# Attention in head pairs with the forget gate added by VectorE, in a two-layer hybrid trunk

## Chip, cores, metric

The kernel runs on one NeuronCore of a Trainium2 chip. The metric is the device time of one execution in microseconds; a kernel is described by the median of its runs.

## What is computed

x is 256 x 1024, in fp32. Layer 0 is an FFN, a gated linear recurrence (RG-LRU) and an FFN; from its result K, V and a forget gate are projected once; layer 1 is an FFN, attention on that K and V, and an FFN. Every block has a norm before and behind it. The change touches the shared K and gate and the attention:

```python
def shared_kv(h, g, w_kv, w_f, b_f):
    hn = rms_norm(h, g)
    kv = (hn @ w_kv).reshape(Bn, S, 2, N_HEADS, HEAD_DIM)          # 16 heads of 64
    ...
    log_f = jax.nn.log_sigmoid((hn @ w_f + b_f).astype(jnp.float32))
    c = jnp.cumsum(log_f, axis=1).transpose(0, 2, 1)
    return k, v, c

def forgetting_attention(xq, w_q, w_o, k, v, c):
    q = (xq @ w_q).reshape(...).transpose(0, 2, 1, 3) * (HEAD_DIM ** -0.5)
    for blk in range(S // Q_BLOCK):                                # two halves of 128 tokens
        ...
        logits = logits + c[:, :, q0:end, None] - c[:, :, None, :end]
        logits = jnp.where(kpos[None, :] <= qpos[:, None], logits, -jnp.inf)
        p = jax.nn.softmax(logits, axis=-1).astype(v.dtype)
        outs.append(jnp.einsum('bhqk,bhkd->bhqd', p, v[:, :, :end]))
    return o @ w_o
```

## The kernel before

**Split products.** Each fp32 weight block of 128 x 1024 is loaded (`load_raw`, five raw buffers, issued by SyncE) and split into an upper part (whi, ScalarE, L199) and a rest (wlo, VectorE, L200), nine such units deep. A product is three matmuls: upper by upper, upper by rest, rest by upper. `mm3` (L207 to L209) does it with the activations still and 512 weight columns moving, once for each half of 128 tokens. `mmj` (L222, L223) does it with 128 x 128 of the weights still and the activations of both token halves moving: 512 columns (upper and rest side by side), then 256. `still` and `tile_items` run `mmj` over four PSUM banks at a time, lent from the pool; `total` then adds the two halves of the banks (a ScalarE copy and a VectorE add).

**Order.** TensorE's order is written out by hand; the order on the other engines is that of a scheduler. A slot is the work of one unit for one token half (six matmuls of 512 columns in the projections). Each slot counts down a list of deferred calls (`defer(n, fn)`), and each prepares the next units.

**PSUM.** `pall` is 8 banks of 128 x 512: 0 to 3 for products, 4 and 5 for logits and small things (`gtbank`), 6 and 7 for transposes (`trbank`). `sparebank` takes what is not lent.

**K and V.** V comes first, in three column blocks, with the 16 gate columns (`v_items`); `running` makes the cumulative gate c (`cq`, and `nck` = -c) out of it. Then K, in two column halves by `proj_items` with L207 to L209 (96 matmuls). `heads_T` (L1015 to L1027) scales a 128 x 512 block into `htok`, puts two more columns beside the 64 of a head (a one, and -c), and transposes four heads at a time into kT, 66 rows high. Q goes the same way, with c and a one, so that the 66-row product of the logits adds the gate by itself.

**Attention.** `attention(t)` is written for a token half t. Half 0 has 4 groups of 4 heads (128 keys), half 1 has 8 groups of 2 heads (256 keys). Step i issues `logits(i)` (L1128, then VectorE's mask L1129 and max L1131, then ScalarE's exps L1136 with their sums), `values(i - 3)` (L1155), `turn(i - 2)` (transposes of the weights pe, L1144, copied to pT by ScalarE, L1146) and, behind every eight heads, `output` (transposes of the normalised result `ot`, L1160 and L1168, split into oh and ol, L1171 and L1172). Successive groups of logits use banks 4 and 5 in turn. The steps are woven into the slots of Q and of the output projection w_o by `ATT_ORDER`: "0" and "1" are slots of a token half, "a0" and "a1" steps of the attention:

```python
    ATT_ORDER = ("0 0 0 0 0 0 0 0 a0 1 a0 1 1 1 a0 1 a0 1 a0 1 a0 a1 1 a0 "
                 "0 a1 a0 a1 0 a1 0 a1 0 a1 0 a1 0 a1 0 a1 0 a1 1 a1 1 a1 1 1 1 1 1 1")
```

The last FFN, ffn_d, follows. L699 is a transpose of the recurrence's parameters, a call deferred by 40 slots in the first FFN.

## Time and profile before

| | us |
|---|---|
| median of 3 runs | 1008.35 (1008.03 to 1010.38) |
| the profiled execution | 1007.29 |
| its span, first to last instruction | 1005.6 |
| TensorE busy | 991.0 |
| VectorE busy | 665.3 |
| ScalarE busy | 566.1 |

TensorE works for nearly the whole span at the full granted clock (mean 0.999). A matmul's record is longer than its distance to the next, since matmuls overlap: costs on TensorE are read from start to start. In the trace a 4-byte matmul of the logits and values counts as two instructions (x8 for four heads).

### The profile page before, as it was taken

To read this page: it belongs to the slowest core of one execution; us is meant where nothing else is said; L and a number is where in the kernel's file an instruction comes from. 1 tells how busy PE (TensorE), PEld (TensorE's weight loads), DVE (VectorE), ACT (ScalarE), POOL (GpSimd) and SP (SyncE) were. 2 spreads that over 40 slices of the span, in tenths; PEclk is the share of its full clock that TensorE was granted. 3 is DMA by queue.
4 is the path that set the end of the run, shared out by engine and by line. 5 is a ranking of instruction groups with operands and counts; after the bars stand their busy time and mean duration, and the time that the engine had idled before them with its cause. 6 is when DMAs were issued, how large, how long until landed. Compare 5 with 4: busy or idle time off the path is not lost.

```text
span 1005.6 us, 13910 instructions
## 1 busy us (share of the span) xinstructions
PE 991.0 (99%) x5302; PEld 847.3 (84%) x5302; DVE 665.3 (66%) x768; ACT 566.1 (56%) x742; POOL 51.5 (5%) x113
## 2 busy tenths in 40 slices
PE   8999999999999999999999999999999999999997
PEld 5887888889988888888898888888888888888885
DVE  5877664568998676664695577674477477666642
ACT  5656543559987555543565555553468566555431
POOL 1500000000003000000000000000020020000000
PEclk9999999999999999999999999999999999999999
DMA  6877656565427666545476766655555057665431
GB/s 230 280 263 204 190 161 197 154 181 151 141 78 250 212 188 187 188 158 185 114 227 218 209 191 184 192 189 168 168 168 168 2 188 237 184 199 195 155 121 42
DMA packets 91864, 178.90 MB, mean 178 GB/s; under 512 B 11790, under 2 KB 31318, under 8 KB 91798
## 3 DMA queue, kind: packets, MB, share of 16 engines
q1 hardware_dynamic: 90550, 176.89, 56.8%
q10 hardware_dynamic: 608, 1.06, 0.3%
q8 instruction: 41, 0.67, 0.3%
q0 software_dynamic: 640, 0.07, 0.1%
q14 instruction: 25, 0.20, 0.1%
HBM read 176.95 MB, written 1.05 MB: 177 GB/s over the span
## 4 chain that ended last, share of the span: by engine, by line
PE 70%; issue 21%; ACT 4%; DVE 4%; POOL 1%; DMA 0%; DVEq 0%; POOLq 0%; ACTq 0%
PE pall L222 21%; PE pall L223 11%; PE pall L209 10%; PE pall L208 10%; PE pall L207 10%; PE pall L845 1%; DVE wlo L200 1%; PE pall L214 1%; PE pall L215 1%; PE pall L216 1%; PE pall L1128 1%; ACT junk L236 1%; PE pall L1155 1%; ACT whi L199 1%; PE pall L1026 1%
## 5 line engine op out<-in xcount | busy, mean ns | idle before, releaser
L200 DVE TENSOR_TENSOR wlo<-raw,whi 128x1024 fp32r<-128x1024 f32 (+4 forms) x329 | 394.6, 1206 | 242.3 <-ACT whi L199 241.8
L199 ACT ACTIVATE whi<-raw 128x1024 fp32r<-128x1024 f32 (+4 forms) x329 | 342.1, 1044 | 290.3 <-PE pall L209 125.6
L222 PE MATMUL pall<-xall,whi 128*128 128x512 f32 x1216 | 424.7, 395 | 0.0
L223 PE MATMUL pall<-xall,wlo 128*128 128x256 f32 x1216 | 338.4, 278 | 0.0
L222 PEld LDWEIGHTS pall<-xall,whi 128*128 128x128 f32 x1216 | 228.1, 188 | 53.3
L223 PEld LDWEIGHTS pall<-xall,wlo 128*128 128x128 f32 x1216 | 228.8, 188 | 0.2
L207 PE MATMUL pall<-whi,hhi 128*128 128x512 f32 (+2 forms) x432 | 166.0, 384 | 0.0
L209 PE MATMUL pall<-whi,hlo 128*128 128x512 f32 (+2 forms) x432 | 165.0, 382 | 0.0
L208 PE MATMUL pall<-wlo,hhi 128*128 128x512 f32 (+2 forms) x432 | 164.8, 382 | 0.0
L209 PEld LDWEIGHTS pall<-whi,hlo 128*128 128x128 f32 x432 | 81.1, 188 | 15.1
L208 PEld LDWEIGHTS pall<-wlo,hhi 128*128 128x128 f32 x432 | 81.2, 188 | 14.7
L207 PEld LDWEIGHTS pall<-whi,hhi 128*128 128x128 f32 x432 | 81.2, 188 | 14.6
L207 PE MATMUL pall<-whi,xall 128*128 128x512 f32 (+2 forms) x168 | 67.1, 400 | 0.1
L208 PE MATMUL pall<-wlo,xall 128*128 128x512 f32 (+2 forms) x168 | 64.9, 386 | 0.4 <-DVE wlo L1226 0.2
L209 PE MATMUL pall<-whi,xall 128*128 128x512 f32 (+2 forms) x168 | 64.9, 386 | 0.1
L229 POOL TENSOR_SCALAR nv<-ss 128x1 f32<-128x1 f32 x24 | 10.9, 453 | 749.8 <-ACT junk L236 749.6
L208 PEld LDWEIGHTS pall<-wlo,xall 128*128 128x128 f32 x168 | 31.7, 189 | 7.5 <-DVE wlo L200 1.2
L209 PEld LDWEIGHTS pall<-whi,xall 128*128 128x128 f32 x168 | 31.5, 188 | 7.1 <-DVE xall L259 1.1
L207 PEld LDWEIGHTS pall<-whi,xall 128*128 128x128 f32 x168 | 31.6, 188 | 5.7 <-ACT xall L254 0.5
L567 ACT ACTIVATE hhi<-prod 128x1024 fp32r<-128x1024 f32 (+1 forms) x21 | 20.6, 980 | 25.2 <-DVE prod L563 25.2
L300 DVE SCALAR_TENSOR_TENSOR t<-pall,rstd,gb 128x512 f32<-128x512 f32 x16 | 11.9, 748 | 26.7 <-ACT junk L236 26.7
L557 ACT ACTIVATE sil<-sil 128x1024 f32<-128x1024 f32 (+1 forms) x21 | 20.6, 982 | 15.1 <-DVE sil L556 15.0
(190 smaller groups left out, 974.2 us busy)
## 6 DMA issues: line engine op xcount, KB each, us to landing
raw<-in_ffn_w_down_dram SPq DMA_DIRECT2D x88, 512.0 KB
raw<-in_ffn_w_up_dram SPq DMA_DIRECT2D x80, 512.0 KB
raw<-in_ffn_w_gate_dram SPq DMA_DIRECT2D x79, 512.0 KB
raw<-in_rg_w_in_dram SPq DMA_DIRECT2D x20, 504.0 KB
raw<-in_rg_w_out_dram SPq DMA_DIRECT2D x10, 504.0 KB
raw<-in_ffn_w_gate_dram SPq DMA_DIRECT2D x18, 256.0 KB
raw<-in_ffn_w_up_dram SPq DMA_DIRECT2D x16, 256.0 KB
raw<-in_w_kv_dram SPq DMA_DIRECT2D x8, 512.0 KB
```

What stands on the lines that cost most here:

```text
L199: nc.scalar.activation(hi[:parts, c:c + m], rawv[:, c:c + m], AF.Copy)
L200: nc.vector.tensor_tensor(lo[:parts, c:c + m], rawv[:, c:c + m], hi[:parts, c:c + m].bitcast(F32), ALU.subtract)
L207: nc.tensor.matmul(ps, xh, wh, start=first, stop=False)
L208: nc.tensor.matmul(ps, xh, wl, start=False, stop=False)
L209: nc.tensor.matmul(ps, xl, wh, start=False, stop=last)
L214: nc.tensor.matmul(ps, wh, xh, start=first, stop=False)
L222: nc.tensor.matmul(pall[:, b, :], wh, xall[:, k, :, :].rearrange("p a b -> p (a b)"), start=k == 0, stop=False)
L223: nc.tensor.matmul(pall[:, b, :S], wl, xhi[:, k, :], start=False, stop=k == 7)
L229: nc.gpsimd.tensor_scalar(v, ss[:, 0:1], ss[:, 1:2] if n == 2 else 0.0, D * EPS * f * f, ALU.add, ALU.add)
L300: nc.vector.scalar_tensor_tensor(t1[n], pf[n], r_in, gb[:, n * 512:(n + 1) * 512], ALU.mult, ALU.mult)
L557: nc.scalar.activation(s, s, AF.Silu)
L567: nc.scalar.activation(hv, pv, AF.Copy)
```

## The change

K is projected by `tile_items`: weights still, the activations z of both halves moving (for that the hidden tile of ffn_b becomes one tile, `hid["all"]`), first into banks 4 to 7 and then into 0 to 3; `total` and a VectorE multiply by the row of norms write kT, now 128 rows (two heads one above the other) by 8 pairs. K is not transposed. Q is transposed in blocks of 128 columns, two heads at a time. The gate no longer rides in the product: `rows(t)` transposes -c, SyncE writes it to a scratch in DRAM and reads it back spread over 128 partitions into `nb` (two DMAs of 128 x 16 x 128, one for each half of the keys; GpSimd then masks the upper half), and VectorE adds c and nb to each head's logits in one operation (L1167). Logits are 64-row matmuls, the two heads of a pair in the two row halves of the array, the one into bank 4 and the other into bank 5, columns 0 to 255 or 256 to 511 in turn. The softmax weights are divided by their sums on VectorE (L1181) before they are turned; in `values` v stands still in column halves and pT moves, so the result comes out transposed and is split into oh and ol (L1207, L1208) at once: `output` and its step go. The recurrence's parameters wait four slots longer.

```diff
--- before
+++ after
     def mmj(b, wh, wl, k, moving):
...
+        both, upper = moving(k)
...
+        nc.tensor.matmul(o, wh, both, start=k == 0, stop=False)
+        nc.tensor.matmul(oh, wl, upper, start=False, stop=k == 7)
...
+    def total(v, b, m):
+        nc.scalar.activation(v, pall[:, b:b + m, S:], AF.Copy)
+        nc.vector.tensor_tensor(v, pall[:, b:b + m, :S], v, ALU.add)
...
-    def heads_T(pool, ps, t, n, scale, cols, dst):
-        if n + t == 0:
-            toks["h"] = pool.tile([P, 16 * HA], F32, tag="prod", name=nm("htok"), bufs=1).rearrange("p (t a b) -> p t a b", t=2, a=8)
-        tok = toks["h"][:, t, :, :]
-        nc.vector.tensor_scalar(tok[:, :, :HD], ps.rearrange("p (a b) -> p a b", a=8), rs[t][:, 0:1], scale,
-                                ALU.mult, ALU.mult)
-        for c, col in enumerate(cols):
-            if col is None:
-                nc.gpsimd.memset(tok[:, :, HD + c:HD + c + 1], 1.0)
-            else:
-                nc.gpsimd.tensor_copy(tok[:, :, HD + c:HD + c + 1], col[:, 8 * n:8 * n + 8].unsqueeze(2))
-        def turn(b):
-            tp = sparebank()
+    def heads_T(pool, ps, t, n, scale, dst):
+        tok = pool.tile([P, 512], F32, tag="htok", name=nm("htok"), bufs=2)
+        nc.vector.tensor_scalar(tok, ps, rs[t][:, 0:1], scale, ALU.mult, ALU.mult)
+        def turn():
+            tp = trbank()
             for j in range(4):
-                nc.tensor.transpose(tp[:HA, j * P:(j + 1) * P], tok[:, 4 * b + j, :], ident)
-            nc.scalar.activation(dst[:, 8 * n + 4 * b:8 * n + 4 * b + 4, :],
-                                 tp[:HA, :].rearrange("p (a b) -> p a b", a=4), AF.Copy)
-        defer(2, lambda: turn(0))
-        defer(3, lambda: turn(1))
+                nc.tensor.transpose(tp[:, j * P:(j + 1) * P], tok[:, j * P:(j + 1) * P], ident)
+            nc.scalar.activation(dst[:, 4 * n:4 * n + 4, :].rearrange("p a b -> p (a b)"), tp, AF.Copy)
+        defer(2, turn)
     def post_k(n):
-        return lambda t, ps: heads_T(pools["f"], ps, t, n, 1.0, (None, kv["nck"][t]), kv["kT"][:, :, t * P:(t + 1) * P])
+        def f(b, m):
+            kk = pools["f"].tile([P, 16 * HA], F32, tag="prod", name=nm("kk"), bufs=1)[:, :1024]
+            v = kk.rearrange("p (a b) -> p a b", a=4)
+            total(v, b, m)
+            nc.vector.tensor_tensor(kv["kT"][:, 4 * n:4 * n + 4, :], v, rcp["v"].unsqueeze(1).to_broadcast([P, 4, S]), ALU.mult)
+        return f
+    def z_moving(k):
+        return kv["z"][:, :, :, k, :], kv["z"][:, 0, :, k, :]
...
     def running(t):
-        pc = gtbank()
+        pc = sparebank()
         if t == 1:
             nc.tensor.matmul(pc[:, :NH], kv["ones"], kv["lf"][0], start=True, stop=False)
         nc.tensor.matmul(pc[:, :NH], kv["triu"], kv["lf"][t], start=t == 0, stop=True)
         nc.vector.tensor_copy(kv["cq"][t], pc[:, :NH])
         nc.vector.tensor_scalar(kv["nck"][t], pc[:, :NH], -1.0, None, ALU.mult)
+        defer(3, lambda: rows(t))
+    def rows(t):
+        pc = sparebank()
+        nc.tensor.transpose(pc[:NH, :P], kv["nck"][t], ident)
+        nc.vector.tensor_copy(kv["ckT"][:, t * P:(t + 1) * P], pc[:NH, :P])
+        if t == 1:
+            nc.sync.dma_start(kv["dram"], kv["ckT"])
...
-        proj_items(A["w_kv"], n * 512, 512, z_x, post_k(n))
+        tile_items(A["w_kv"], n * 512, 4 - 4 * n, post_k(n), z_moving)
...
+        nb = att["nb"] = ap.tile([P, NH, S], F32, name="nb")
+        src = kv["dram"].rearrange("h k -> (h k)").partition_broadcast(P).rearrange("p (h k) -> p h k", h=NH)
+        for k in range(2):
+            nc.sync.dma_start(nb[:, :, k * P:(k + 1) * P], src[:, :, k * P:(k + 1) * P])
+        nc.gpsimd.affine_select(out=nb[:, :, P:], in_=nb[:, :, P:], compare_op=ALU.is_ge, fill=NEG, base=0,
+                                pattern=[[0, NH], [-1, P]], channel_multiplier=1)
+        att["q"] = [ap.tile([P, 8, P], F32, name=f"qT{t}") for t in range(2)]
         ap.tile([P, 32], F32, name="pad")
...
         per = 4 // nk
-        mask = kv["cmask"].unsqueeze(1).to_broadcast([P, per, P])
+        np_ = per // 2
+        w = nk * P
         box = {}
         G = NH // per
+        def head(hg, b, j):
+            return 2 * (hg * np_ + j) + b
         def logits(hg):
-            hds = range(hg * per, (hg + 1) * per)
-            ps = gtbank().rearrange("p (a b) -> p a b", a=per)
-            for j, hd in enumerate(hds):
-                nc.tensor.matmul(ps[:, j, :], att["q"][t][:, hd, :], kv["kT"][:, hd, :nk * P], start=True, stop=True)
-            nc.vector.tensor_tensor(ps[:, :, t * P:], ps[:, :, t * P:], mask, ALU.add)
-            mx = spool.tile([P, 4], F32, tag="mx", name=nm("mx"))
-            nc.vector.tensor_reduce(mx[:, :per], ps, AX.X, ALU.max, negate=True)
-            if hds[0] % 8 == 0:
-                box["sm"] = spool.tile([P, 8], F32, tag="sm", name=nm("sm"))
-            pe = ap.tile([P, per, nk * P], F32, tag="pe", name=nm("pe"), bufs=3)
-            for j, hd in enumerate(hds):
-                nc.scalar.activation(pe[:, j, :], ps[:, j, :], AF.Exp, bias=mx[:, j:j + 1],
-                                     accum_out=box["sm"][:, hd % 8:hd % 8 + 1])
-            box["pe", hg], box["s", hg] = pe, box["sm"]
+            c = (hg % 2) * S
+            lg = pall[:, 4:6, c:c + S]
+            for j in range(np_):
+                for b in range(2):
+                    p = hg * np_ + j
+                    nc.tensor.matmul(lg[:, b, j * w:(j + 1) * w], att["q"][t][b * HD:(b + 1) * HD, p, :],
+                                     kv["kT"][b * HD:(b + 1) * HD, p, :w], start=True, stop=True)
+            for b in range(2):
+                for j in range(np_):
+                    hd = head(hg, b, j)
+                    v = lg[:, b, j * w:(j + 1) * w]
+                    nc.vector.scalar_tensor_tensor(v, v, kv["cq"][t][:, hd:hd + 1], att["nb"][:, hd, :w], ALU.add, ALU.add)
+            if t == 0:
+                v = lg.rearrange("p b (j k) -> p b j k", j=2)
+                nc.vector.tensor_tensor(v, v, kv["cmask"].unsqueeze(1).unsqueeze(1).to_broadcast([P, 2, 2, P]), ALU.add)
+            mx = spool.tile([P, 4], F32, tag="mx", name=nm("mx"))[:, :per]
+            nc.vector.tensor_reduce(mx, lg.rearrange("p b (j k) -> p b j k", j=np_), AX.X, ALU.max, negate=True)
+            sm = spool.tile([P, 4], F32, tag="sm", name=nm("sm"))[:, :per]
+            pe = box["pe", hg] = ap.tile([P, per, w], F32, tag="pe", name=nm("pe"), bufs=3)
+            for b in range(2):
+                for j in range(np_):
+                    i = b * np_ + j
+                    nc.scalar.activation(pe[:, i, :], lg[:, b, j * w:(j + 1) * w], AF.Exp, bias=mx[:, i:i + 1],
+                                         accum_out=sm[:, i:i + 1])
+            nc.vector.reciprocal(sm, sm)
+            nc.vector.tensor_tensor(pe, pe, sm.unsqueeze(2).to_broadcast([P, per, w]), ALU.mult)
         def turn(hg):
             tp = trbank()
             nc.scalar.activation(pT.rearrange("p a b -> p (a b)"), tp, AF.Copy)
         def values(hg):
-            hds = range(hg * per, (hg + 1) * per)
-            if hds[0] % 8 == 0:
+            p0 = hg * np_
+            if p0 % 4 == 0:
                 box["po"] = mmbank()
-            po, pT, sm = box["po"], box["pT", hg], box["s", hg]
-            for j, hd in enumerate(hds):
+            po, pT = box["po"], box["pT", hg]
+            for j in range(np_):
+                o = (p0 + j) % 4 * P
                 for k in range(nk):
-                    nc.tensor.matmul(po[:, (hd % 8) * HD:(hd % 8 + 1) * HD], pT[:, j * nk + k, :],
-                                     kv["v"][k][:, hd * HD:(hd + 1) * HD], start=k == 0, stop=k == nk - 1)
-            if hds[-1] % 8 == 7:
-                nc.vector.reciprocal(sm, sm)
-                ot = box["ot", hds[-1] // 8] = ap.tile([P, 8, HD], F32, tag="ot", name=nm("ot"), bufs=2)
-                nc.vector.tensor_tensor(ot, po.rearrange("p (a b) -> p a b", a=8),
-                                        sm.unsqueeze(2).to_broadcast([P, 8, HD]), ALU.mult)
+                    for b in range(2):
+                        hd = head(hg, b, j)
+                        nc.tensor.matmul(po[b * HD:(b + 1) * HD, o:o + P], kv["v"][k][:, hd * HD:(hd + 1) * HD],
+                                         pT[:, (b * np_ + j) * nk + k, :], start=k == 0, stop=k == nk - 1)
+            if (p0 + np_) % 4 == 0:
+                b = (p0 + np_) // 4 - 1
+                oh_v = att["oh"][t][:, 4 * b:4 * b + 4, :].rearrange("p a b -> p (a b)")
+                ol_v = att["ol"][t][:, 4 * b:4 * b + 4, :].rearrange("p a b -> p (a b)")
+                nc.scalar.activation(oh_v, po, AF.Copy)
+                nc.vector.tensor_tensor(ol_v, po, oh_v.bitcast(F32), ALU.subtract)
                 release(po)
-        def output(b):
-            otv = box["ot", b].rearrange("p a b -> p (a b)")
-            tp = trbank()
-            for j in range(4):
-                nc.tensor.transpose(tp[:, j * P:(j + 1) * P], otv[:, j * P:(j + 1) * P], ident)
-            oh_v = att["oh"][t][:, 4 * b:4 * b + 4, :].rearrange("p a b -> p (a b)")
-            ol_v = att["ol"][t][:, 4 * b:4 * b + 4, :].rearrange("p a b -> p (a b)")
-            nc.scalar.activation(oh_v, tp, AF.Copy)
-            nc.vector.tensor_tensor(ol_v, tp, oh_v.bitcast(F32), ALU.subtract)
         steps = []
-        for i in range(G + 4):
+        for i in range(G + 3):
             s = []
             if i < G:
                 s.append(lambda i=i: logits(i))
                 s.append(lambda i=i: values(i - 3))
             if 0 <= i - 2 < G:
                 s.append(lambda i=i: turn(i - 2))
-            j = i - 4
-            if j >= 0 and (j + 1) * per % 8 == 0:
-                s.append(lambda j=j: output((j + 1) * per // 8 - 1))
             steps.append(s)
         return steps
...
-                 "0 a1 a0 a1 0 a1 0 a1 0 a1 0 a1 0 a1 0 a1 0 a1 1 a1 1 a1 1 1 1 1 1 1")
+                 "0 a1 0 a1 0 a1 0 a1 0 a1 0 a1 0 a1 0 a1 1 a1 1 a1 1 1 1 1 1 1")
...
-    defer(40, rg_params)
+    defer(44, rg_params)
...
-    run(n_kv)
+    run_ffn((n_v, n_kv, n_kv))
```

### Where it moves instructions

First place: TensorE in the first token half. Before, from the first logits (L1128) to the second; kT and qT are K and Q transposed, whi, wlo and xall the operands of a slot.

```order
L1128 MATMUL pall<-kT,qT_6471 128x128 x4
L207 MATMUL pall<-whi_6282,xall 128x512
L208 MATMUL pall<-wlo_6283,xall 128x512
L209 MATMUL pall<-whi_6282,xall 128x512 [waits DVE_49]
...
L1128 MATMUL pall<-kT,qT_6471 128x128 [waits Activation_49]
L1128 MATMUL pall<-kT,qT_6471 128x128 x3
```

The wait of the second logits here is for the copy into qT. After, the same stretch:

```order
L1161 MATMUL pall<-kT,qT_6470 128x128 [waits Activation_49]
L1161 MATMUL pall<-kT,qT_6470 128x128 x3
L207 MATMUL pall<-whi_6275,xall 128x512
L208 MATMUL pall<-wlo_6276,xall 128x512
L209 MATMUL pall<-whi_6275,xall 128x512 [waits DVE_49]
...
L1161 MATMUL pall<-kT,qT_6470 128x128 [waits DVE_49,Activation_49]
L1161 MATMUL pall<-kT,qT_6470 128x128 [waits Activation_49]
L1161 MATMUL pall<-kT,qT_6470 128x128 x2
```

The qT of both is written ahead of the first logits now; the waits of the second on ScalarE are for the second and the fourth exp of the first group, which read the banks that these matmuls write.

Second place: VectorE between the max of the second group (mx) and that of the third. Before:

```order
L1131 TENSOR_REDUCE mx_6602<-pall 128x4 [waits DVE_49]
L1158 RECIPROCAL sm_6579<-sm_6579 128x8 [waits Activation_49]
L1015 TENSOR_SCALAR htok_6527<-pall,rstd_6517 128x8x64 [waits PE_49,Pool_49]
L200 TENSOR_TENSOR wlo_6625<-raw_6622,whi_6624 128x1024 [waits DMAHW1_49,Activation_49]
L1129 TENSOR_TENSOR pall<-pall,cmask 128x512 [waits PE_49]
L200 TENSOR_TENSOR wlo_6642<-raw_6639,whi_6641 128x1024 [waits DMAHW2_49,Activation_49]
L200 TENSOR_TENSOR wlo_6657<-raw_6654,whi_6656 128x1024 [waits DMAHW4_49,Activation_49]
L1131 TENSOR_REDUCE mx_6665<-pall 128x4 [waits DVE_49]
```

After:

```order
L1172 TENSOR_REDUCE mx_6603<-pall 128x4 [waits DVE_49]
L200 TENSOR_TENSOR wlo_6629<-raw_6626,whi_6628 128x1024 [waits DMAHW2_49,Activation_49]
L1180 RECIPROCAL sm_6605<-sm_6605 128x4 [waits Activation_49]
L1181 TENSOR_TENSOR pe_6606<-pe_6606,sm_6605 128x512 [waits DVE_49]
L1027 TENSOR_SCALAR htok_6650<-pall,rstd_6516 128x512 [waits PE_49,Pool_49]
L200 TENSOR_TENSOR wlo_6641<-raw_6638,whi_6640 128x1024 [waits DMAHW6_49,Activation_49]
L200 TENSOR_TENSOR wlo_6655<-raw_6652,whi_6654 128x1024 [waits DMAHW7_49,Activation_49]
L1167 SCALAR_TENSOR_TENSOR pall<-pall,cq_2932,nb 128x128 [waits PE_49] x2
L1167 SCALAR_TENSOR_TENSOR pall<-pall,cq_2932,nb 128x128 [waits DVE_49] x2
L200 TENSOR_TENSOR wlo_6692<-raw_6689,whi_6691 128x1024 [waits DMAHW0_49,Activation_49]
L1170 TENSOR_TENSOR pall<-pall,cmask 128x2x256 [waits DVE_49]
L1172 TENSOR_REDUCE mx_6667<-pall 128x4 [waits DVE_49]
```

Between the two maxima stand now a multiply, four gate adds and one split more.

Third place: TensorE at the start of the second half of K, after the change (whi and wlo are units of K, hid holds z; before, slots of L207 to L209 with blocks of L1026 stood here).

```order
L233 MATMUL pall<-hid_3062,wlo_4710 128x256
L232 MATMUL pall<-hid_3062,whi_4722 128x512 [waits Activation_49]
L233 MATMUL pall<-hid_3062,wlo_4723 128x256
L232 MATMUL pall<-hid_3062,whi_4722 128x512
...
L232 MATMUL pall<-hid_3062,whi_4722 128x512 [waits DVE_49]
...
L1076 MATMUL pall<-ident,nck_2931 16x128 [waits DVE_49]
L232 MATMUL pall<-hid_3062,whi_4722 128x512
```

The transpose of the second `rows` stands behind eight matmuls of the second half, in a bank out of which `total` still adds the first half (its wait on VectorE).

More of the change, by code (lines that the diff above doesn't have):

```diff
@@ L545, in post_up @@
             return f
-        def total(v, b, m):
-            nc.scalar.activation(v, pall[:, b:b + m, S:], AF.Copy)
-            nc.vector.tensor_tensor(v, pall[:, b:b + m, :S], v, ALU.add)
         def gate_rows(b, m):
@@ L604, in work @@
                 def work(t, u, k0=k0):
[L605 removed]
+                    still(u, k0, 4)
                     if k0 == 6:
```

71 lines of the change are left out of this document (40 added, 31 removed).

## The prediction

> **What bounds the kernel now.** I read the busy lines first, then TensorE's waits, then the stretches of the attention, then single rows.
>
> ```profile
> PE 991.0 (99%) x5302; PEld 847.3 (84%) x5302; DVE 665.3 (66%) x768; ACT 566.1 (56%) x742; POOL 51.5 (5%) x113
> PE pall L699 <- issue: 2.1, 1, 2.1
> ...
> PE pall L1155 <- ACT pT L1146: 0.3, 1, 0.3
> ```
>
> TensorE is busy for 99% of a span of 1005.6 us. In the second view (us in total, times, longest us) the attention owns one wait of 0.3 us: it costs only what TensorE executes. So the change can gain by removing matmuls and by the 2.1 us at L699, and it loses whatever it makes TensorE wait for. The next table (stretch, length, busy us of PE, PEld, DVE, ACT, POOL, granted clock, DMA share, GB/s) covers the attention:
>
> ```profile
> 745.00:765.00 20.00, 20.00 (x127) 17.31 (x126) 12.04 (x16) 14.24 (x38) 0.24 (x2) 1.00 0.33 99
> 765.00:785.00 20.00, 19.93 (x128) 17.30 (x128) 13.06 (x21) 13.33 (x38) 0.24 (x2) 1.00 0.43 133
> 785.00:805.00 20.00, 19.69 (x125) 17.42 (x124) 8.51 (x15) 10.83 (x29) 0.87 (x2) 1.00 0.00 1
> ```
>
> VectorE and ScalarE work 43 to 71% of the time there, unnoticed, because each softmax has some microseconds of matmuls to hide behind. The sum below is made against this execution's 1007.29 us; the median of the runs, 1008.35, is 1.1 us above it, and I add the sum to the median.
>
> **The change, part by part.**
>
> A. The gate's parameter transpose (L699) stands 33 matmuls later.
>
> ```profile
> 82.01 0.39 PE L222 MATMUL pall<-xall,whi 128*128 128x512 f32 x1
> ...
> 82.36 0.39 PE L222 MATMUL pall<-xall,whi 128*128 128x512 f32 x1
> ...
> 85.00 0.27 PE L699 MATMUL pall<-ident,prow 88*126 88x88 f32 x1 [2.13 <-issue]
> ```
>
> A pair L222 + L223 takes 0.35 us (82.01 to 82.36), so 33 matmuls are 5.8 us, more than the wait: **-2.1**. If the wait only moved, 0.
>
> B. K with still weights. 96 matmuls of 0.23 us (start to start, as from 748.91 to 749.14 under D) become 64 pairs of 0.35 us: 22.1 against 22.4, +0.3. Eight blocks of four transposes go:
>
> ```profile
> 755.53 0.60 PE L1026 MATMUL pall<-ident,htok 128*66 128x128 f32 x4
> 755.88 0.47 PE L207 MATMUL pall<-whi,xall 128*128 128x512 f32 x1
> ```
>
> 0.35 us to the next start, and that matmul is 0.09 us longer than usual: 8 x 0.44 = -3.5. Two small transposes (rows(t)) cost some 0.3. But the second stands behind only eight matmuls (1.4 us) of the second half of K, and it writes into a bank that the first half of K still holds. It waits for VectorE's add, and the order shows what lies ahead of that: on ScalarE a split that starts only when the last-but-one matmul of the first half is done, then the copy; on VectorE the split of the same unit, then the add.
>
> ```profile
> L199 ACT ACTIVATE whi<-raw 128x1024 fp32r<-128x1024 f32 x284 | 299.4, 1058 | 272.7 <-PE pall L209 115.6 <-PE pall L222 96.7 <-issue 46.6
> L549 ACT ACTIVATE prod<-pall 128x1024 f32<-128x1024 f32 x17 | 17.2, 1009 | 1.8 <-PE pall L223 1.8
> L200 DVE TENSOR_TENSOR wlo<-raw,whi 128x1024 fp32r<-128x1024 f32 x284 | 345.5, 1222 | 229.5 <-ACT whi L199 229.0
> L550 DVE TENSOR_TENSOR prod<-pall,prod 128x1024 f32<-128x1024 f32 x17 | 20.7, 1217 | 1.6 <-ACT prod L549 1.6
> ```
>
> 1.06 + 1.22 + 1.22 = 3.5, minus 1.4: a new stall of 2.1 (0.8 if the split is early: 1.01 + 1.22 - 1.4). B together: **-0.8** (-2.1 to -0.6).
>
> C. Q's transposes: two blocks per 512 columns become one. One such block less stands ahead of the first logits: **-0.4**. The other savings of this kind lie inside D, where a wait decides.
>
> D. First token half. Up to now logits of successive groups went to alternate banks. Now each group writes both banks 4 and 5, and the order shows logits(i+1) waiting for the exps of group i; six matmuls stand between. That takes away the cover on which the 99% rest. Rows of before, TensorE and ScalarE:
>
> ```profile
> 748.91 0.39 PE L209 MATMUL pall<-whi,xall 128*128 128x512 f32 x1
> 749.14 1.05 PE L1128 MATMUL pall<-kT,qT 66*128 66x128 f32 x8
> 749.95 0.48 PE L207 MATMUL pall<-whi,xall 128*128 128x512 f32 x1
> ...
> 751.42 1.06 PE L1128 MATMUL pall<-kT,qT 66*128 66x128 f32 x8
> ...
> 757.40 1.16 PE L1128 MATMUL pall<-kT,qT 66*128 66x128 f32 x8
> ...
> 760.22 1.05 PE L1128 MATMUL pall<-kT,qT 66*128 66x128 f32 x8
> ...
> 769.36 1.03 PE L1128 MATMUL pall<-kT,qT 66*128 66x256 f32 x4
> ...
> 793.24 1.03 PE L1128 MATMUL pall<-kT,qT 66*128 66x256 f32 x4
> ```
>
> ```profile
> 751.62 1.06 ACT L199 ACTIVATE whi<-raw 128x1024 fp32r<-128x1024 f32 x1 [3.07 <-PE pall L209]
> 752.69 1.28 ACT L1136 ACT_TABLE_LOAD   x1
> 753.99 0.37 ACT L1136 ACTIVATE pe<-pall,mx 128x128 f32<-128x128 f32 x1
> ...
> 755.28 0.21 ACT L1136 ACTIVATION_READ_ACCUMULATOR pe<-pall,mx 128x1 f32 x1
> ```
>
> Before, the exps of group 0 ran from 4.85 to 6.35 us after logits(0) began (T = 749.14), and logits(1) started at +2.28, four microseconds before they were done. The same split and table load stand before them in the changed order, so logits(1) cannot end before +6.8 (before +3.1). VectorE's part fits in that time; its prices:
>
> ```profile
> L803 DVE SCALAR_TENSOR_TENSOR xc<-pall,par,xc 126x255 f32<-126x255 f32 x10 | 4.7, 472 | 0.0
> L300 DVE SCALAR_TENSOR_TENSOR t<-pall,rstd,gb 128x512 f32<-128x512 f32 x16 | 11.9, 748 | 26.7 <-ACT junk L236 26.7
> L1129 DVE TENSOR_TENSOR pall<-pall,cmask 128x512 f32<-128x512 f32 x4 | 2.8, 695 | 1.0 <-PE pall L1128 0.9
> L1131 DVE TENSOR_REDUCE mx<-pall 128x2 f32<-128x512 f32 x8 | 5.5, 688 | 0.2
> L1160 DVE TENSOR_TENSOR ot<-pall,sm 128x512 f32<-128x512 f32 x4 | 2.8, 689 | 1.4 <-PE pall L1155 1.4
> L1136 ACT ACTIVATE pe<-pall,mx 128x256 f32<-128x256 f32 x16 | 7.4, 471 | 1.1 <-DVE mx L1131 1.1
> ```
>
> ```profile
> 756.92 0.20 DVE L1158 RECIPROCAL sm<-sm 128x8 f32<-128x8 f32 x1 [1.98 <-ACT pe L1136]
> ```
>
> No row has the new gate add. Between 255 columns (0.47) and 512 (0.75) lies a slope that gives 0.34 for 128 columns and 0.47 for 256; I bound it by 0.30 (the same line through the mask) and 0.47. Group 1: multiply of group 0 until +7.25, four adds 1.36, mask 0.70, reduce 0.69 until +10.0, four exps until +11.6; then the next qT copy (0.6), for which logits(2) wait: **+12.2** against +8.26 before. Logits(3) wait for the exps of group 2, and VectorE has ahead of those: split 1.22, reciprocal and multiply until +12.5, htok 0.75, two splits 2.44, four adds 1.36, another split 1.22, mask and reduce 1.38: +19.6; the first two exps end at +20.5, the others at +21.2. TensorE has been out of work since +14.8. Logits(3) are at **+20.5** against +11.08. To the first logits of the other token half there remain 7.6 us of matmuls and about 1 us of waiting for pT and the multiply: **+29.5** against +20.22 before. D: **+9.2** (+6 to +11; the low end if the three splits find their way around the chain, as the order denies).
>
> E. Second half, eight groups. VectorE's order per group is reciprocal, add, multiply, add, reduce: 0.20 + 0.47 + 0.69 + 0.47 + 0.69 = 2.5; with the exps ahead (0.47 + 0.47 + 0.21) the ring closes after 3.65, plus 0.69 where an ol split stands in it. Before, the seven distances add up to 23.88 (769.36 to 793.24), two of them short since nothing chained them. Now 4.6 for the first (12 matmuls stand there as before), 3.9, and five of 3.65 + 0.69: 27.5. E: **+3.6** (0 to +5; at 0 the adds run below the rows).
>
> F. Behind the last logits two blocks of output transposes go (-0.9, by the 0.44 of B), and values in column halves may run side by side:
>
> ```profile
> 764.42 1.00 PE L1155 MATMUL pall<-v,pT 128*128 128x64 f32 x8
> 765.26 0.61 PE L1144 MATMUL pall<-ident,pe 128*128 128x128 f32 x4
> ```
>
> Eight such passes take 0.84 us to the next start, so halves side by side save 0.42 per block, four blocks 1.6; I take half of it and 0.5 us for a wait on the direct oh and ol: **-1.2** (+0.5 to -2.5).
>
> Whether halves run side by side no row shows: a pass of 64 columns (105 ns) is no shorter than one of 128 (101 ns, 749.14 to 749.95 for eight), so serial halves cost what full passes did. The Trainium skill, "TensorEngine Tiling (Array Packing)", Key Properties, says that tiles run in parallel, but also that changing the tiling mode drains the TensorE; no run here shows that. By the first half the sum would be 2 to 3 us lower, by the second higher, as rival 4 works out.
>
> Sum: -2.1 - 0.8 - 0.4 + 9.2 + 3.6 - 1.2 = **+8.3** on 1007.29 (1015.6), on the median 1008.35: **1016.6**, rounded to 1016.5.
>
> **Rivals.**
>
> 1. *The waits are covered and the matmuls decide.* L699 -2.1; B without its stall -2.9; eight Q blocks become four, -1.8; four blocks of output transposes, -1.8; halves of the logits up to -5 and of the values -5: about -19, **989**. For it: TensorE is at 99%, so every matmul counts. Against it: the exps of group 0 end at +6.35 in a row of before, and the order makes logits(1) wait for them. Chance 0.05. With half the waiting of D and E, -6.4: -6 less some halves, about **1001 to 1006**, 0.15.
>
> 2. *The spread tile is late* (the slower end). SP issues it behind ffn_c's last matmul, some 13.6 us ahead of the first add (735.75 to 749.99, less C and some), and the w_o weights and the gain queue behind it.
>
> ```profile
> 735.75 0.39 PE L209 MATMUL pall<-whi,hlo 128*128 128x512 f32 x1
> ```
>
> ```profile
> q1 hardware_dynamic: 90550, 176.89, 56.8%
> ```
>
> 90550 packets hold 16 engines for 571 us each, so 0.10 us for a packet of 1950 bytes. The tile is 4096 rows of 512 bytes: by packets 26 us, by bytes 6.7. At the first price the w_o weights land some 5 us after ScalarE needs them, and their splits stand ahead of pT and the exps in its order: **1021**. It decides from about 0.06 us per packet. Chance 0.15.
>
> 3. *The clock drops in the pauses.* In the pause of 2.13 us at L699 the granted clock stays 1.00; D has one of 3.3 us (+2.3 to +5.6, where two exps are done) and one of 5.7, longer than any here. Half a clock for as long as the pause lasted would cost 1.5 to 3 us: **1019**. The Trainium skill, "TensorE: Matmul & The Clock Gate", What's actually happening, has the clock halve after an idle window of about 3.4 us; L699 agrees as far as it goes. Chance 0.1.
>
> 4. *Each change between full and half tiles empties TensorE.* Twelve logits and twelve values blocks change it and change it back, 48 changes; by what a matmul outlasts its pitch (0.39 - 0.23 = 0.16) 7.7 us, of which the waits of D and E hide the half that belongs to the logits: +3.8, **1020**. No row speaks for or against it. Chance 0.05.
>
> **How the numbers follow.** Forecast 0.5 (1011 to 1020, at 1016.5); rival 2 0.15; rival 3 0.1; rival 4 0.05; rival 1 0.05 and its milder form 0.15. The range, 1004 to 1023, leaves out rival 1's full form, the lower half of the milder one, and a sum of several of 2 to 4. A measurement of this kernel tells about 0.3% (3 us) from no change: faster than 1005.3, 0.05 and 0.08 of the milder form; from there to 1011.4 the rest of it and 0.06 of the forecast, 0.13; slower, 0.74.
>
> **What would show it.** A: no wait at L699. B: a wait of about 2 us at L1076 on VectorE's add. D: waits at L1161 on ScalarE's pe, together 8 to 10 us, the longest, 5 to 6 us, before logits(3). E: logits of the second half 3.6 to 4.4 us apart. If TensorE's waits at L1161 add up to less than 3 us I am wrong about the banks; if ScalarE's L199 waits for DMAs around the first logits, rival 2; if the clock column falls below 1.00 there, rival 3. It would be wrong altogether if the waits are there and the end still comes earlier: then halves side by side saved more than I gave them.

## The result, and the profile after

The changed kernel takes 1024.33 us (median of three runs, 1021.49 to 1026.52) against 1009.36 us before: ratio 1.0147, 95% interval 1.0110 to 1.0183. It is slower by about 15 us, where 8 were forecast and the range ended at 1023. A fourth run, the one that was profiled, had 0.84 of the clock from end to end (1103.77 us) and is left out, so the lines below come from a second profile of the same kernel (run `again`: 1022.86 us, span 1021.1).

Its busy line and TensorE's waits (us in total, times, longest):

```profile
PE 993.4 (97%) x5272; PEld 839.6 (82%) x5272; DVE 682.6 (67%) x810; ACT 563.0 (55%) x732; POOL 49.1 (5%) x98
PE pall L1161 <- ACT pe L1178: 12.0, 5, 4.9
PE pall L1076 <- DVE kk L517: 2.0, 1, 2.0
PE pall L151 <- DVE idle L137: 1.5, 1, 1.5
PE pall L232 <- DVE ckT L1077: 1.2, 1, 1.2
```

The wait at the parameter transpose is gone from the list. In its place stand 12.0 us ahead of logits, on ScalarE's exps, and two waits in K, of which one was forecast (L1076, 2.0 against 2.1) and one was not (L232).

The logits of the changed kernel (start, duration, the idle time ahead and what ended it), first half and the first and last of the second:

```profile
747.94 0.72 PE L1161 MATMUL pall<-kT,qT 64*128 64x128 f32 x8
...
753.51 1.92 PE L1161 MATMUL pall<-kT,qT 64*128 64x128 f32 x8 [3.27 <-ACT pe L1178]
...
762.07 0.72 PE L1161 MATMUL pall<-kT,qT 64*128 64x128 f32 x8
...
769.66 1.91 PE L1161 MATMUL pall<-kT,qT 64*128 64x128 f32 x8 [4.90 <-ACT pe L1178]
...
780.68 0.70 PE L1161 MATMUL pall<-kT,qT 64*128 64x256 f32 x4
...
808.06 1.67 PE L1161 MATMUL pall<-kT,qT 64*128 64x256 f32 x4 [2.09 <-ACT pe L1178]
```

Counted from the first logits they stand at +5.6, +14.1, +21.7 and +32.7 (before +2.3, +8.3, +11.1, +20.2). Look at the durations too: eight passes take 0.72 us in two of the rows and 1.9 in the other two, the ones behind a pause. The table of stretches says why (the third column from the right is the granted clock):

```profile
745.00:765.00 20.00, 16.50 (x78) 12.32 (x76) 12.81 (x22) 10.37 (x26) 2.02 (x1) 0.83 0.48 161
765.00:785.00 20.00, 15.29 (x84) 11.02 (x84) 14.27 (x26) 10.52 (x30) 0.00 (x0) 0.83 0.43 131
785.00:805.00 20.00, 18.27 (x104) 12.08 (x105) 13.32 (x30) 8.50 (x26) 0.00 (x0) 1.00 0.10 28
805.00:825.00 20.00, 17.80 (x103) 13.16 (x100) 12.22 (x21) 11.45 (x24) 1.89 (x5) 0.83 0.12 30
```

Three of the four have lost 17% of their clock. In stretches of one microsecond, around the first pause:

```profile
752.00:753.00 1.00, 0.00 (x0) 0.00 (x0) 0.59 (x1) 0.99 (x3) 0.00 (x0) 0.84 0.00 0
753.00:754.00 1.00, 0.49 (x2) 0.49 (x2) 0.00 (x0) 1.00 (x8) 0.00 (x0) 0.50 0.63 74
...
758.00:759.00 1.00, 1.00 (x6) 0.92 (x5) 0.00 (x0) 0.68 (x1) 0.00 (x0) 0.50 0.00 0
759.00:760.00 1.00, 1.00 (x5) 0.81 (x5) 0.59 (x1) 1.00 (x6) 0.00 (x0) 0.75 0.00 0
760.00:761.00 1.00, 1.00 (x6) 0.83 (x5) 0.81 (x2) 1.00 (x6) 0.00 (x0) 1.00 0.00 0
```

The clock falls to 0.50 at about 752.7, near the end of the pause (TensorE is idle until 753.51), and is back at 759.5, 6.8 us later: six of those microseconds are work, at half speed. The other two drops are as long, 769.7 to 776.6 and 807.3 to 814.1.

Where the time went, by marks on TensorE (spans of the two profiled executions):

| stretch | before | after | difference | forecast |
|---|---|---|---|---|
| to the first slot of V (A) | 501.8 | 500.4 | -1.4 | -2.1 |
| V, K, ffn_c (B) | 234.2 | 234.7 | +0.5 | -0.8 |
| ffn_c's end to the first logits (C) | 13.2 | 12.8 | -0.4 | -0.4 |
| to the first logits of the second half (D) | 20.2 | 32.7 | +12.5 | +9.2 |
| to its last logits (E) | 23.9 | 27.4 | +3.5 | +3.6 |
| to ffn_d's first slot (F) | 21.7 | 22.7 | +0.9 | -1.2 |
| ffn_d | 190.6 | 190.4 | -0.2 | 0 |
| sum | 1005.6 | 1021.1 | +15.5 | +8.3 |

### The profile page after: what moved, and what is told of

Read it like the earlier page. It is cut to its first block, busy times and chain, and to the rows that moved or that the text cites. A ratio compares the mean times of both kernels' runs of the same rounds, so it can differ in the third digit from the quotient of the medians.

```text
span 1102.0 us, 13863 instructions
## 1 busy us (share of the span) xinstructions
PE 1076.0 (98%) x5272; PEld 875.6 (79%) x5272; DVE 686.5 (62%) x810; ACT 568.5 (52%) x732; POOL 48.5 (4%) x98
## 4 chain that ended last, share of the span: by engine, by line
PE 75%; issue 19%; DVE 2%; ACT 1%; DMA 1%; POOL 0%; DVEq 0%; POOLq 0%; ACTq 0%
PE pall L232 22%; PE pall L233 11%; PE pall L207 11%; PE pall L209 11%; PE pall L208 11%; PE pall L855 2%; PE pall L214 1%; PE pall L215 1%; PE pall L216 1%; PE pall L1161 1%; DVE wlo L200 1%; PE pall L255 1%; DMA raw<-in_w_kv_dram 1%; PE pall L1201 1%; PE pall L1187 1%
## 5 line engine op out<-in xcount | busy, mean ns | idle before, releaser
L232 PE MATMUL pall<-xall,whi 128*128 128x512 f32 x1216 | 458.4, 416 | 0.0
L233 PE MATMUL pall<-xall,wlo 128*128 128x256 f32 x1216 | 357.5, 294 | 0.0
L232 PEld LDWEIGHTS pall<-xall,whi 128*128 128x128 f32 x1216 | 233.9, 192 | 66.8
L233 PEld LDWEIGHTS pall<-xall,wlo 128*128 128x128 f32 x1216 | 235.3, 193 | 0.2
L207 PE MATMUL pall<-whi,hid 128*128 128x512 f32 (+2 forms) x400 | 163.6, 409 | 0.0
L209 PE MATMUL pall<-whi,hid 128*128 128x512 f32 (+2 forms) x400 | 163.0, 408 | 0.0
L208 PE MATMUL pall<-wlo,hid 128*128 128x512 f32 (+2 forms) x400 | 162.8, 407 | 0.0
L209 PEld LDWEIGHTS pall<-whi,hid 128*128 128x128 f32 x400 | 76.7, 192 | 20.9
L207 PEld LDWEIGHTS pall<-whi,hid 128*128 128x128 f32 x400 | 77.0, 192 | 20.5
L208 PEld LDWEIGHTS pall<-wlo,hid 128*128 128x128 f32 x400 | 76.6, 191 | 20.5
L207 PE MATMUL pall<-whi,xall 128*128 128x512 f32 (+2 forms) x168 | 72.2, 430 | 0.0
L209 PE MATMUL pall<-whi,xall 128*128 128x512 f32 (+2 forms) x168 | 69.6, 414 | 0.1
L209 PEld LDWEIGHTS pall<-whi,xall 128*128 128x128 f32 x168 | 32.8, 195 | 9.3 <-DVE xall L269 0.8
L207 PEld LDWEIGHTS pall<-whi,xall 128*128 128x128 f32 x168 | 32.9, 196 | 8.8 <-ACT xall L264 0.5
L602 ACT ACTIVATE hid<-prod 128x1024 fp32r<-128x1024 f32 (+1 forms) x21 | 20.6, 980 | 19.5 <-DVE prod L598 19.5
L246 ACT ACTIVATE junk<-pall,rf 128x512 bf16<-128x512 f32 x16 | 10.9, 683 | 34.6 <-PE pall L209 34.6
```

The lines of the kernel that those rows point to most:

```text
L207: nc.tensor.matmul(ps, xh, wh, start=first, stop=False)
L208: nc.tensor.matmul(ps, xh, wl, start=False, stop=False)
L209: nc.tensor.matmul(ps, xl, wh, start=False, stop=last)
L232: nc.tensor.matmul(o, wh, both, start=k == 0, stop=False)
L233: nc.tensor.matmul(oh, wl, upper, start=False, stop=k == 7)
L602: nc.scalar.activation(hv, pv, AF.Copy)
```

## The experiments

The theory: the waits that the order shows, plus a clock drop behind each long pause. Rivals: that changes between full and half tiles cost the time; that pauses have nothing to do with the clock; that VectorE's load as such, not the order, decides.

**again**, the changed kernel itself.

> The changed kernel as it is, for a profile at the full clock. Theory (waits and clock): of the 16 us over the kernel before, the waits at L1161 for ScalarE's exps make 10 to 12, the two waits around rows(t) in K 4 to 5, and the granted clock falls below 1.00 in the attention and around those waits alone, worth 4 to 6 us; the matmuls left out give back the rest. Rival (tile changes): the clock stays at 1.00 and the blocks of logits and values take longer from start to start than the full-width blocks of before, 0.81 and 0.84 us.

1024.22 us, ratio 1.0147 (1.0118 to 1.0177). The waits are 12.0 us ahead of logits and 3.2 in K, where 4 to 5 were expected in K; the drops are those above, all in the attention and none behind the waits in K. The blocks speak against the rival (a logits block of the first half between its neighbours, then a values block of the second half and the transposes behind it):

```profile
747.61 0.40 PE L209 MATMUL pall<-whi,xall 128*128 128x512 f32 x1
747.94 0.72 PE L1161 MATMUL pall<-kT,qT 64*128 64x128 f32 x8
748.58 0.50 PE L207 MATMUL pall<-whi,xall 128*128 128x512 f32 x1
...
797.41 0.66 PE L1201 MATMUL pall<-pT,v 128*64 128x128 f32 x8
798.00 0.66 PE L1187 MATMUL pall<-ident,pe 128*128 128x128 f32 x4
```

0.64 and 0.59 us to the next start, where the full-width blocks took 0.81 and 0.84. The changes are not free: the matmul ahead of the logits block takes 0.33 us to the next start (0.23 before), and the one behind it lasts 0.50 (0.48 before). Even with these some 0.12 us, the stretch of block and neighbours is shorter than before (1.31 us from the matmul ahead to the second one behind, 1.36 before). At the full clock the tiles do not lengthen the attention.

**sbuf**: the gate add writes into SBUF, and the banks come free behind it.

```diff
-                    nc.vector.scalar_tensor_tensor(v, v, kv["cq"][t][:, hd:hd + 1], att["nb"][:, hd, :w], ALU.add, ALU.add)
+                    nc.vector.scalar_tensor_tensor(pe[:, b * np_ + j, :], v, kv["cq"][t][:, hd:hd + 1], att["nb"][:, hd, :w], ALU.add, ALU.add)
```

Mask, max and exps then work in pe.

> The gate add writes its sum into the tile pe in SBUF, and mask, max and exps work there; so the next logits wait for the adds and no longer for the exps. Theory (waits and clock): the waits at L1161 fall from 11 us to under 3, the clock stays up, and the time falls by 9 to 14 us, to 1011 to 1016. Rival (tile changes): the waits fall but the blocks keep their length; the time falls by less than 6 us.

1010.47 us, ratio 1.0004 (0.9988 to 1.0019): 13.7 us faster than the changed kernel. VectorE and ScalarE are busy as long as before the edit (679.9 and 563.6 us, against 682.6 and 563.0), so VectorE's load as such was not what cost the time. What is left of TensorE's waits in the attention:

```profile
PE pall L1161 <- DVE pe L1168: 2.9, 1, 2.9
...
PE pall L1200 <- ACT pT L1188: 1.5, 1, 1.5
```

The 12.0 us of waits ahead of logits became 2.9, with 1.5 ahead of values, and three drops one (760.8 to 767.6, at the pause of 2.9; the expectation had none). In the second half the logits now follow each other as TensorE's own work allows:

```profile
786.32 0.70 PE L1161 MATMUL pall<-kT,qT 64*128 64x256 f32 x4
789.51 0.70 PE L1161 MATMUL pall<-kT,qT 64*128 64x256 f32 x4
792.71 0.70 PE L1161 MATMUL pall<-kT,qT 64*128 64x256 f32 x4
```

3.2 us a step, with 3.66 in the changed kernel and 3.55 before. This settles that the shared banks, held until the exps are done, were the cause of the waits ahead of logits.

**busy**: matmuls that nobody reads ahead of logits 2 and 4 of the first half. The waits stay; TensorE is only not idle.

```diff
             lg = pall[:, 4:6, c:c + S]
+            if t == 0 and hg in (1, 3):
+                fill = trbank()
+                for _ in range(12 if hg == 1 else 20):
+                    nc.tensor.matmul(fill, xhi[:, 0, :P], xhi[:, :4, :P], start=True, stop=True)
```

> Twelve matmuls of 512 columns that nobody reads are put ahead of the second logits of the first half and twenty ahead of the fourth, into the pauses of 3.3 and 4.7 us. Theory (waits and clock): the end of the chain is where it was, but the clock holds at 1.00 there: 2 to 4 us faster than the changed kernel. If pauses have no part in the clock: no change within 1.5 us, or up to 2 us slower where the filler outlasts the pause.

1021.23 us, ratio 1.0114 (1.0097 to 1.0130): by the medians 3 us faster although TensorE executes 32 matmuls more, but the interval overlaps that of `again`, and the profile has to carry the argument. The two filled pauses and the one that was left:

```profile
753.00:757.00 4.00, 3.48 (x16) 2.54 (x14) 2.98 (x5) 3.17 (x7) 0.33 (x1) 1.00 0.47 189
765.00:771.00 6.00, 5.38 (x24) 4.11 (x22) 5.42 (x9) 1.97 (x5) 0.00 (x0) 1.00 0.68 205
808.00:812.00 4.00, 4.00 (x18) 2.76 (x19) 2.34 (x5) 0.64 (x3) 0.00 (x0) 0.57 0.00 0
```

The clock holds at 1.00 in both and falls in the third (808.5 to 811.9), behind a pause of 2.09 us that was not filled. In this execution it fell once more, behind the pause of 2.0 us in K. Pauses lower the clock: shown. What the two drops had cost can be read from the logits of this run, the first of which start at 751.46:

```profile
763.15 0.71 PE L1165 MATMUL pall<-kT,qT 64*128 64x128 f32 x8
771.35 0.48 PE L1165 MATMUL pall<-kT,qT 64*128 64x128 f32 x2 [0.97 <-ACT pe L1182]
...
780.49 0.70 PE L1165 MATMUL pall<-kT,qT 64*128 64x256 f32 x4
```

The second logits stand at +5.6 as in the changed kernel, but the later ones at +11.7, +19.9 and +29.0 in place of +14.1, +21.7 and +32.7: the two drops cost 3.7 us.

**late**: `defer(3, lambda: rows(t))` becomes `defer(24, ...)`.

> rows(t) is deferred by 24 slots in place of 3, into ffn_c. Theory (waits and clock): the waits of 2.6 us at L232 on ckT and of 1.9 us at L1076 on kk go, 4 to 5 us faster than the changed kernel, one more if the clock had dropped there. Rival: the weights ring had let the other engines fall behind and the same time is lost a few slots later, less than 1.5 us faster.

1020.45 us, ratio 1.0116 (1.0092 to 1.0141): 3.8 us by the medians (4 to 5 were expected), with intervals that overlap. Both K waits are gone from the list. V and K together take 48.0 us instead of 51.9 (500.5 to 548.5; 500.4 to 552.3), so the waits and their surroundings cost 3.9. The agreement with the 3.8 in the total is partly chance: in the profiled execution ffn_c took 2.5 us and ffn_d 1.9 us longer, for a reason told at the end, and one drop fewer occurred. The pause of 2.09 us ahead of the last logits is there, but the clock stays at 1.00 behind it:

```profile
806.40 1.15 PE L1161 MATMUL pall<-kT,qT 64*128 64x256 f32 x4 [2.09 <-ACT pe L1178]
```

From these logits to ffn_d it takes 20.1 us, with 22.7 in `again`, so that drop cost 2.5; in busy, with a drop of 3.4 us there, it takes 21.7.

**fix** = sbuf + late.

> The sum in SBUF and rows(t) 24 slots later together. If the waits in K and in the attention are independent, the savings add: 13.7 and 3.8 us off 1024.2 give 1006.7, 2 us faster than the kernel before. If they share a cause (the other engines run behind from K on), less than 15.5 us off, 1009 or more.

1005.78 us, ratio 0.9974 (0.9965 to 0.9983), 18 us below the changed kernel: the savings add, and it is the first version that is faster than the kernel before, by 0.3%.

**serial**: fix, with the loops over halves (b) and over pairs or key blocks exchanged, so that two passes of the same half follow each other.

> As fix, with the two halves of the array not in turn: both matmuls of the upper row half, then those of the lower, and in values both passes of a column half one behind the other. If halves run side by side because they alternate, a block of logits of the first half grows from 0.64 us to 0.81 and one of values of the second half from 0.59 to 0.84. If the shorter blocks have another cause (less to load for half a tile), they stay at 0.64 and 0.59.

1005.51 us, ratio 0.9966 (0.9956 to 0.9976). The blocks keep their length (two of this run's):

```profile
747.29 0.72 PE L1161 MATMUL pall<-kT,qT 64*128 64x128 f32 x8
747.94 0.50 PE L207 MATMUL pall<-whi,xall 128*128 128x512 f32 x1
...
786.74 0.66 PE L1200 MATMUL pall<-pT,v 128*64 128x128 f32 x8
787.34 0.65 PE L1186 MATMUL pall<-ident,pe 128*128 128x128 f32 x4
```

0.65 and 0.60. The shorter blocks do not hang on halves in turn; a pass of half a tile is simply shorter (0.08 us against 0.10). The prediction had reckoned that halves one behind the other cost what full passes did; they do not. Why, these runs do not settle.

**fix_order**: fix, with one slot more between logits 3 and 4 of the first half.

```diff
-    ATT_ORDER = ("0 0 0 0 0 0 0 0 a0 1 a0 1 1 1 a0 1 a0 1 a0 1 a0 a1 1 a0 "
-                 "0 a1 0 a1 0 a1 0 a1 0 a1 0 a1 0 a1 0 a1 1 a1 1 a1 1 1 1 1 1 1")
+    ATT_ORDER = ("0 0 0 0 0 0 0 0 a0 1 a0 1 1 1 a0 1 1 a0 1 a0 1 a0 a1 0 a0 "
+                 "0 a1 0 a1 0 a1 0 a1 0 a1 0 a1 0 a1 1 a1 1 a1 1 a1 1 1 1 1 1")
```

> As fix, and one slot more between the third and the fourth logits of the first half, taken from behind (a slot of w_o of the first half fills the place it leaves). The wait of 2.9 us there and the half clock that follows it go: 3 to 5 us faster than fix if the clock drop belongs to that wait, 1.4 us (a slot's six matmuls) to 2.9 if it does not; no gain if VectorE is simply behind by its work and the wait moves to the next step.

1009.13 us, ratio 1.0009 (1.0000 to 1.0018): 3.3 us slower than fix; the expectation had a gain or no change. The wait moved and grew:

```profile
PE pall L1186 <- DVE pe L1180: 3.6, 1, 3.6
...
PE pall L1161 <- DVE pe L1168: 1.1, 1, 1.1
```

The turn of the next step now waits for the multiply: VectorE is behind by its queue, and a slot put ahead of it only moves the place where TensorE meets it. In the two profiles this makes the first half 1.5 us longer (25.9 us from its first logits to those of the second half, 24.3 in fix); another 1.6 us are lost between the first and last logits of the second half, whose slots the edit also puts in another order.

**fix_pool** (the multiply on GpSimd, `nc.vector` to `nc.gpsimd` in one line) and **fix_mask** (that, and the gate tile of heads 8 to 15 masked beforehand by GpSimd).

> As fix, with the multiply by 1/sum on GpSimd in place of VectorE: 12 x 0.69 us off VectorE. If VectorE's queue ahead of the fourth logits is what sets the wait, it shrinks by two multiplies, 1.4 us, and the time by 1.5 to 3; if GpSimd takes longer than VectorE did, turn waits for it instead and the kernel is 1 to 4 us slower than fix.

> As fix_pool, and for heads 8 to 15 of the first half the gate tile is masked beforehand by GpSimd (a second tile), so that two of the four mask additions of 0.69 us leave VectorE. If VectorE's load sets the wait at the fourth logits, 0.5 to 1.5 us less wait than fix_pool; if the two splits ahead of its gate adds set it, the wait stays at 2.6 us.

fix_pool 1004.65 us, ratio 0.9965 (0.9953 to 0.9977): no difference to fix beyond the intervals, so neither of the two outcomes expected. fix_mask 1003.14 us, 0.9944 (0.9929 to 0.9959). The wait at logits 4 is 2.9 us in fix and 2.6 in both of these: taking 1.4 us of multiplies off VectorE shortened it by 0.3, as expected if two splits set it. In the profiles of both, two splits (756.8 to 759.4 in fix_pool, 757.0 to 759.6 in fix_mask) stand right ahead of the last gate add, behind which the logits start. Why fix_mask is 1.5 us faster than fix_pool stays open: in its profile the waits on pT ahead of values (1.8 us in fix_pool) are gone and the drop lasts 3.4 us in place of 6.8.

**fill**: fix, with eleven matmuls that nobody reads in the one long wait that is left; **best**: fix_mask with the same.

> As fix, with eleven matmuls that nobody reads ahead of the fourth logits, in the one long wait that is left (2.9 us). If that wait lowers the clock, the drop to 0.50 behind it goes and 1 to 2 us with it; if the drop comes from something else, it stays, and the time is that of fix within 1 us.

> fix_mask with the eleven filler matmuls of fill. If the clock drop behind the last long wait is worth what fill suggests (1 to 2 us), 1 to 2 us faster than fix_mask, a ratio to the kernel before of 0.993; if fill was faster than fix by chance, no difference to fix_mask (0.9944).

fill 1004.73 us, ratio 0.9958 (0.9942 to 0.9975), fix 0.9974: in the direction and size expected, with intervals that overlap. In its profile the drop is gone (the same stretch of fill and of fix):

```profile
760.00:764.00 4.00, 3.97 (x30) 3.11 (x30) 3.97 (x10) 1.56 (x6) 0.00 (x0) 1.00 0.97 321
```

```profile
760.00:764.00 4.00, 3.97 (x24) 3.12 (x25) 3.96 (x10) 1.13 (x4) 0.00 (x0) 0.69 0.91 289
```

The first half, from its first logits to those of the second, takes 23.1 us in fill, 24.3 in fix with a drop of 3.4 us, and 25.4 in sbuf with a drop of 6.8 at the same place.

best takes 1002.89 us, ratio 0.9938 (0.9925 to 0.9952), not told apart from fix_mask. It is the fastest of these kernels, 6 us below the one before.

**rg40**: fix, with `defer(40, rg_params)`.

> As fix, with rg_params deferred by 40 again. If the later place is what removed the wait of 2.1 us at the parameter transpose, that wait is back and the kernel is 2 us slower than fix; if the wait had gone for another reason, no difference.

1007.47 us, ratio 0.9988 (0.9977 to 0.9999), 1.7 us slower than fix by the medians, with intervals that overlap, and the wait is back where it was:

```profile
86.48 0.27 PE L709 MATMUL pall<-ident,prow 88*126 88x88 f32 x1 [2.12 <-issue]
```

In that execution the clock fell behind it, for 3.4 us (87.0 to 90.5); behind the same pause of the kernel before it had not.

## Why the prediction was wrong

**The sign and the waits were right; the step that failed is the price of the clock in the pauses.** The sum counted each pause at its length and put the clock behind it at nothing. The drop stood apart, as rival 3: "Half a clock for as long as the pause lasted would cost 1.5 to 3 us", with a chance of 0.1. The drops came. They lasted 6.83 us each, longer than their pauses, and began near the end of these, so they fell on the work behind. Behind the first pause, logits(1) took 1.84 us to the next start in place of 0.64, six matmuls 0.43 each in place of 0.23, a block of transposes 0.70 in place of 0.35. The runs in which drops are missing give the price: 3.7 us for the two in D (busy) and 2.5 for the one in F (late), together 6.2 of the 7.2 us by which the sum fell short (+8.3 against +15.5). The prediction's one row on the clock was the pause of 2.13 us at L699, behind which it stayed at 1.00; rg40 has a drop behind the same pause, so that row could not carry the low chance.

- **A** (-2.1, measured -1.4). The transpose no longer waits, and rg40 shows that the place is the cause. Of the 0.7 that is missing, 0.5 lies in the wait for the first load of x at L255 (1.1 us in this execution, 0.6 before).
- **B** (-0.8, measured +0.5). The stall at L1076 was right (2.0). Missed was its sibling: the first rows(t) leaves its transpose in a bank that K's first half takes over a few slots later, and the matmul L232 waits until VectorE, behind its splits, has copied ckT (1.2 us here, 2.7 in another run). The bank that an added operation *leaves* occupied was not followed.
- **C** (-0.4) came out.
- **D** (+9.2, measured +12.5). The waits were right. With the clock held in busy, the marks stand at +5.6, +11.7, +19.9 and +29.0, against +5.6, +12.2, +20.5 and +29.5 worked out, and D comes to +8.8 (the prediction's own 29.5 less 20.22 is 9.3). Only the wait that it had ahead of logits(2) did not appear. VectorE's queue up to the third max ran as the order was added up:

```profile
759.41 1.22 DVE L200 TENSOR_TENSOR wlo<-raw,whi 128x1024 fp32r<-128x1024 f32 x1 [1.49 <-ACT whi L199]
760.80 0.18 DVE L1180 RECIPROCAL sm<-sm 128x4 f32<-128x4 f32 x1 [0.17 <-ACT pe L1178]
761.01 0.69 DVE L1181 TENSOR_TENSOR pe<-pe,sm 128x512 f32<-128x512 f32 x1
762.25 0.75 DVE L1027 TENSOR_SCALAR htok<-pall,rstd 128x512 f32<-128x512 f32 x1 [0.54 <-PE pall L209]
762.92 2.35 DVE L200 TENSOR_TENSOR wlo<-raw,whi 128x1024 fp32r<-128x1024 f32 x2
765.18 1.13 DVE L1167 SCALAR_TENSOR_TENSOR pall<-pall,cq,nb 128x128 f32<-128x128 f32 x4
766.22 1.21 DVE L200 TENSOR_TENSOR wlo<-raw,whi 128x1024 fp32r<-128x1024 f32 x1
767.35 0.69 DVE L1170 TENSOR_TENSOR pall<-pall,cmask 128x512 f32<-128x512 f32 x1
768.08 0.69 DVE L1172 TENSOR_REDUCE mx<-pall 128x4 f32<-128x512 f32 x1
```

  The 3.3 us too few are the two drops (3.7), less the 0.4 by which the rest came out shorter.
- **The gate add's price** held: 0.34 and 0.47 us were read off a slope between two other widths; the rows have 352 and 487 ns.

```profile
L1167 DVE SCALAR_TENSOR_TENSOR pall<-pall,cq,nb 128x256 f32<-128x256 f32 x16 | 7.6, 487 | 1.3 <-PE pall L1161 0.7
L1167 DVE SCALAR_TENSOR_TENSOR pall<-pall,cq,nb 128x128 f32<-128x128 f32 x16 | 4.9, 352 | 0.1
```

- **E** (+3.6, measured +3.5): the ring of 3.65 us per group ran at 3.65 to 3.66 in the four distances that it governs alone.
- **F** (-1.2, measured +0.9): the third drop lies here (807.3 to 814.1). Without it, in late, F is 20.1 us, -1.6 against before. A values block is 0.25 us shorter (0.21 estimated), about half of which the changes of tile around it take back.
- **Rival 1** is refuted by the 12.0 us of waits. **Rival 2** did not come about, though not by much: the two DMAs of the spread tile were issued at 735.6, GpSimd's mask, which waits for the second of them, started at 747.6, and VectorE's first gate add at 748.72, right behind its htok. That is 12 us for the tile, with 6.7 and 26 as the two prices. ScalarE's splits around the first logits waited for TensorE's release of a unit, not for weights. **Rival 4**: refuted as a slowdown by the blocks above; a block pays some 0.12 us for its two changes, where 0.32 were reckoned, and is still shorter than before.

## What to carry to other kernels

When TensorE is at 99%, look at what keeps a buffer: here one write target (PSUM in place, or a tile in SBUF) decided whether the next logits waited for two operations or for the whole softmax, worth 13.7 us. Price a pause of TensorE of two microseconds and more at its length plus what a clock drop may cost behind it; here that was 1.2 to 1.6 us for a drop of 3.41 us and 1.9 to 2.5 for one of 6.83. And where an added operation borrows a bank, follow the bank until its reader is done, on the engine whose queue that reader stands in.

## What the runs showed of the hardware

**The clock.** Drops lasted 3.41 or 6.83 us wherever TensorE still had work. Pauses of 2.6 to 4.9 us ahead of logits or turns were all followed by one, but one of 2.67 us in K (busy, at L232) was not. Pauses of 2.0 to 2.1 us were in some profiles (the third of `again` and of busy, the one in K of busy, rg40) and not in others (the kernel before, the third of late, the one in K of `again` and sbuf). In rg40 even a pause of 1.65 us at the start of the kernel was.

Where a pause falls accounts for part of this. Within an execution the drops start whole multiples of 3.413 us apart: 5.00 and 16.00 of them in `again` (752.68, 769.74, 807.29), 77.00 in busy, 23.00 and 222.00 in rg40. Cut the span into pieces of that length at these points: each of the 13 pieces in which TensorE, at the full clock, was idle for 1.85 us or more is followed by a drop, and none with less than 1.3; between the two, some are and some are not (the 1.83 of the kernel before is not). The 2.67 us of busy lie 1.08 and 1.58 in two pieces, the 2.09 of late 1.18 and 0.90, the 2.09 of busy in one. What makes a drop last one piece or two stays open. The Trainium skill, "TensorE: Matmul & The Clock Gate", What's actually happening, has a free-running window of 3413 ns, with which the lengths and the distances agree; it also asks for a whole idle window, and 1.85 us within one were enough here.

The time goes with the clock: the four executions of `again` had a mean granted clock of 0.993, 0.989, 0.986 and 0.986 and took 1021.06, 1022.86, 1025.59 and 1028.00 us.

**Two paces.** The pair L222 + L223 (L232 + L233 after) runs at 0.3466 us in some stages and at 0.3533 in others, at a granted clock of 1.00 in both and without a wait. A stage mostly keeps its pace for tens of microseconds and more. In ffn_c the kernel before, `again`, busy and sbuf ran at the first. late, fix and the seven kernels made from fix ran at the second, two of them for a part of the stage; over the whole stage that is 352 x 0.0067 = 2.4 us. So it may be a price of the later rows(t); with one such profile for each kernel this is not shown. In other stages the pace does not go with that edit. What sets it stays open. It is why the profiles of two kernels can differ by 2 us in a stage that neither touches.
